# A decoder trunk's first norm: squares of a token-major copy on ScalarE in place of GpSimd's sums

## The chip, the cores and the metric

The kernel runs on one core of a Trainium2 chip. The metric is device time in microseconds (us): the median of three runs of the kernel before is 846.38 us (846.37 to 846.58). The engines are TensorE (PE, matmuls; PEld is its weight load), VectorE (DVE), ScalarE (ACT), GpSimd (POOL) and SyncE (SP), which issues most DMAs.

## The reference

One layer on x of 256 tokens by 2048 channels, all float32:

```
h = x * rsqrt(mean(x*x over channels) + 1e-6) * norm_w
proj = h @ w_in                     # 2048 x 14864: all inputs of three mixers, and gate logits
o_a, o_b, o_c = three token mixers of width 1024, each times silu of its own gate path
x = x + sum over n of sigmoid(gates[n]) * (o_n @ w_out[n])
out = rmsnorm(x, final_norm_w)
```

The change is in the first line: in how the mean of squares is made, and in how the scaled input gets to TensorE.

## The kernel before

**Numbers in two parts.** TensorE multiplies in float32r. So that float32 accuracy is kept, each operand is split: a high part (a cast to float32r) and a low part (the rest). A product takes three passes: high by high, high by low, low by high. For weights ScalarE casts (`whi<-raw`, L412) and VectorE subtracts (`wlo<-raw,whi`, L414), 1024 columns at a time; here such a half of a weight tile is called a step, h0, h1, h2 and so on. `split(h)` emits both, and once both halves of a tile are split the load of the tile three further on is issued on SP (`load`, L359): three buffers of 1 MB hold raw weights (`RB`), four hold split halves (`WB`), and `part(h)`, where TensorE takes step h, emits the split of step h + 3.

**The input.** `xT` is loaded channel-major into `xc_t`: 16 tiles of 128 channels by 256 tokens. `hT` holds x * norm_w in two parts, tile by tile; 1/rms is not in it, but is multiplied into results later (`rstd` along tokens in a row, `rtok` with tokens on partitions). `chunk(q)` makes four tiles of `hT`: ScalarE multiplies two of them and casts (ACTIVATE `hT<-xc_t,pr`), VectorE multiplies the other two into `boh`, ScalarE casts these, and VectorE makes the low parts: `low(k)` for the first two (SCALAR_TENSOR_TENSOR `hT<-xc_t,pr,hT`), one subtraction of 128x512 for the others (`hT<-boh,hT`). The first four tiles go by twos (`first_chunk`): a product and cast on ScalarE, and `low`, for each tile.

**The first block** (`chan_pair`) computes 512 columns of `w_in` (kind CC, inputs of the third mixer) in steps h0 to h7, eight of them, while the input still comes in; a step has 24 matmuls of 256 columns (L479). `squares(q)` is called in it for each quarter of the input: GpSimd squares four tiles and adds them up into `ssum`.

**The norm** (`norm_stream`): TensorE sums `ssum` over partitions, once with a matrix of ones (256 columns, the sum in all partitions) and twice into one column (tokens on partitions); ScalarE makes exp(-ln/2); VectorE refines it into `rstd`; GpSimd raises the column form to the power -1/2 (`rtok`).

**What sets the order.** Each engine executes its instructions in the order in which they were written. TensorE's blocks stand in a fixed order (`PLAN`); what is to be done between them (norm, mixers, emptying of accumulators) are generators, from which `Streams` takes pieces whenever a model of the engines' times (`Clock`, `Engine.cost`) says that a piece's inputs are there. So a change of one piece moves pieces behind it. A block's accumulators have two buffers (`pp`, `st.room()`): the third block needs those of the first, which `padded` empties, and that needs `rstd`. `branch_out(n)` holds the split outputs of a mixer (`boh`, `bol`), which the output projection of that mixer reads.

Of the kernel before, what the change touches and what calls it, by code (L numbers as in the profile page):

```python
# [281 lines left out]
def trunk(ctx, tc, xT, xtok, w, wdt, wax, prm, heads, cst, msk, fnw, out):  # L282
    nc = tc.nc
    PSUM = bass.MemoryType.PSUM
    consts = ctx.enter_context(tc.tile_pool(name="consts", bufs=1))
    big = ctx.enter_context(tc.tile_pool(name="big", bufs=1))
    wpool = ctx.enter_context(tc.tile_pool(name="wpool", bufs=WB))
    bop = ctx.enter_context(tc.tile_pool(name="bop", bufs=2))
# [24 lines left out]
    xc_t = big.tile([P, KD, S], F32, tag="x16", name="xc_t")  # L313
# [30 lines left out]
    def flag(name):  # L344
        flags[name] = max(ck.end, ck.after)
# [22 lines left out]
    x_there = []  # L368
# [29 lines left out]
    def split(h):  # L398
        if h >= 2 * NTILES or h in split_done:
            return  # L400
        split_done.add(h)
        raw = raws[h // 2]
        sl = slice((h % 2) * 1024, (h % 2) * 1024 + 1024)
        if h < LASTH:
            hi = wpool.tile([P, 1024], F32R, name="whi")
            lo = wpool.tile([P, 1024], F32R, name="wlo")
            ck.after = max(there[h], done.get(h - WB, 0.0))
        else:
            hi = fin["pool"].tile([P, 1024], F32R, name="whj", bufs=4)
            lo = fin["pool"].tile([P, 1024], F32R, name="wlj", bufs=4)  # L410
            ck.after = there[h]
        nc.scalar.copy(out=hi, in_=raw[:, sl])  # L412
        t = ck.run("act", 0.97)
        nc.vector.tensor_tensor(out=lo, in0=raw[:, sl], in1=hi.bitcast(F32), op=ALU.subtract)  # L414
        t = ck.run("dve", 1.15, t)
        parts[h] = (hi, lo, t)
        ck.after = ck.end = 0.0
        if h % 2:
            del raws[h // 2]
            load(h // 2 + RB, t)  # L420
            if h // 2 == 1:
# [17 lines left out]
    hT = big.tile([P, KD, 2, S], F32R, name="hT")  # L439
# [43 lines left out]
    def chan_pair():  # L483

        st.room()
        both = pp.tile([P, 2, 512], F32, name="ps")
        pss = [both[:, b].rearrange("p (c s) -> p c s", c=2) for b in range(2)]
        for u in (0, 1):
            first_split(u)
            first_chunk(u)  # L490
        split(1)
        chunk(1)
        for h in range(2, WB - 1):
            split(h)
        for q in range(4):
            for b in range(2):
                h = 2 * q + b
                if h in (5 - WB, 7 - WB):
                    chunk(2 + (h + WB - 5) // 2)
                hi, lo = part(h)  # L500
                if b == 0:
                    squares(q)
                ck.t["pe"] = max(ck.t["pe"], xs_at[q])
                first_quarter(pss[b], q, hi, lo, h)
        return pss
# [44 lines left out]

    rstd = consts.tile([P, 1, S], F32, name="rstd")
    rtok = consts.tile([P, 2, 2], F32, name="rtok")
    ssum = m1.tile([P, S], F32, tag="yg", name="ssum")
    rv = m1.tile([P, 2, S], F32, tag="br", name="rv")

    def chunk(q):

        x = xc_t[:, 4 * q:4 * q + 4]
        hi, lo = hT[:, 4 * q:4 * q + 4, 0], hT[:, 4 * q:4 * q + 4, 1]
        ck.after = x_there[q + 1]  # L560
        y = bop.tile([P, 2, S], F32, name="boh")
        for kk in range(2):
            act.activation(out=hi[:, kk], in_=x[:, kk], func=AF.Copy, scale=pc("norm_w", 4 * q + kk))
            dve.tensor_scalar(out=y[:, kk], in0=x[:, 2 + kk], scalar1=pc("norm_w", 4 * q + 2 + kk), scalar2=None, op0=ALU.mult)
        ck.after = ck.end
        act.copy(out=hi[:, 2:4], in_=y)
        for kk in range(2):
            low(4 * q + kk)
        ck.after = ck.end
        dve.tensor_tensor(out=lo[:, 2:4], in0=y, in1=hi[:, 2:4].bitcast(F32), op=ALU.subtract)  # L570
        xs_at[q] = ck.end
        ck.after = ck.end = 0.0

# [12 lines left out]
    def squares(q):
        x = xc_t[:, 4 * q:4 * q + 4]
        sq = bop.tile([P, 4, S], F32, name="bol")
        ck.after = x_there[q + 1]
        gpe.tensor_tensor(out=sq, in0=x, in1=x, op=ALU.mult)  # L590
        gpe.tensor_tensor(out=sq[:, 0:2], in0=sq[:, 0:2], in1=sq[:, 2:4], op=ALU.add)
        if q == 0:
            gpe.tensor_tensor(out=ssum, in0=sq[:, 0], in1=sq[:, 1], op=ALU.add)
        else:
            gpe.tensor_tensor(out=sq[:, 0], in0=sq[:, 0], in1=sq[:, 1], op=ALU.add)
            gpe.tensor_tensor(out=ssum, in0=ssum, in1=sq[:, 0], op=ALU.add)
        ck.after = ck.end = 0.0

    xs_at = {}

    def norm_stream():

        yield from st.get("pm", "p")
        ms = pm.tile([P, 512], F32, name="pmt")
        mm.matmul(ms[:, :S], lhsT=ones, rhs=ssum, start=True, stop=True)
        for j in range(2):
            mm.matmul(ms[:, S + j:S + j + 1], lhsT=ssum[:, j * P:(j + 1) * P], rhs=ones[:, 0:1], start=True, stop=True)
        yield "av"
        r0, v = rv[:, 0], rv[:, 1]
        act.activation(out=r0, in_=ms[:, :S], func=AF.Ln, scale=1.0 / D, bias=eps)  # L610
        act.activation(out=r0, in_=r0, func=AF.Exp, scale=-0.5)

        yield "v"
        dve.scalar_tensor_tensor(out=v, in0=ms[:, :S], scalar=D * EPS, in1=r0, op0=ALU.add, op1=ALU.mult)
        dve.tensor_scalar(out=rtok[:, 0], in0=ms[:, S:S + 2], scalar1=1.0 / D, scalar2=EPS, op0=ALU.mult, op1=ALU.add)
        st.put("pm")
        dve.scalar_tensor_tensor(out=v, in0=v, scalar=-0.5 / D, in1=r0, op0=ALU.mult, op1=ALU.mult)
        dve.scalar_tensor_tensor(out=rstd[:, 0], in0=v, scalar=1.5, in1=r0, op0=ALU.add, op1=ALU.mult)
        flag("rstd")
        half = m1.tile([P, 2], F32, name="half")  # L620
        gp.memset(half, -0.5)
        gp.tensor_tensor(out=rtok[:, 0], in0=rtok[:, 0], in1=half, op=ALU.pow)
        gp.tensor_scalar(out=rtok[:, 1], in0=rtok[:, 0], scalar1=0.5, scalar2=None, op0=ALU.mult)
        flag("rtok")


    rcoef = consts.tile([P, 8], F32, name="rcoef")
# [828 lines left out]
```

## Time and profile before

| | |
|---|---|
| median of 3 runs | 846.38 us |
| profiled execution | 848.2 us, of which its span (first to last instruction) 846.4 us |
| mean granted clock of TensorE | 0.994 |
| TensorE busy | 827.4 us, 98% of the span, 4953 matmuls |
| VectorE, ScalarE, GpSimd busy | 637.3, 475.2, 35.9 us |
| DMA | 159.08 MB, mean 188 GB/s |

Times in rows are from the span's start. A row of the timeline may merge equal instructions that follow each other (xN); its square bracket is the idle time before it and what ended it. Matmuls overlap, so their pace is read from starts. [...] The last 14.3 us of the span are the end of the final norm and the output's DMAs.

### The profile page before, as it was taken

How to read it: one execution, taken by the hardware profiler on the slowest of the kernel's cores; microseconds unless marked ns; L12 is line 12 of the kernel's file. 1: busy time of each engine (PE TensorE's matmuls, PEld its weight loads, DVE VectorE, ACT ScalarE, POOL GpSimd, SP SyncE). 2: the span in 40 equal slices, each digit the busy share in tenths (PEclk: the TensorE clock that was granted, in tenths of full speed). 3: DMA queues.
4: the chain of work that ended last, by engine and by line, in shares of the span. 5: the costliest groups of instructions: out<-in, count | busy, mean ns of one | idle time of the engine just before them, and what ended most of it. 6: DMA issues, size and time to landing. Idle time of an engine off the chain costs nothing.

```text
span 846.4 us, 12476 instructions
## 1 busy us (share of the span) xinstructions
PE 827.4 (98%) x4953; PEld 702.1 (83%) x4953; DVE 637.3 (75%) x961; ACT 475.2 (56%) x647; POOL 35.9 (4%) x58
## 2 busy tenths in 40 slices
PE   6899999999999999999999999999999999999995
PEld 6888888878888888888888888888888888888885
DVE  7978888787879768668668778778878877566463
ACT  4466455645564755746656556746656665544443
POOL 6301000000000000000100000000000000000000
PEclk9999999999999999999999999999999999999998
DMA  8537564754545545554554445545544554655532
GB/s 302 197 127 256 173 218 150 310 181 168 199 168 194 203 185 195 199 198 150 204 196 180 171 150 202 196 151 199 180 169 155 194 198 151 248 192 179 195 131 100
DMA packets 24618, 159.08 MB, mean 188 GB/s; under 512 B 2816, under 2 KB 3360, under 8 KB 6768
## 3 DMA queue, kind: packets, MB, share of 16 engines
q1 hardware_dynamic: 23072, 151.53, 50.1%
q0 software_dynamic: 1344, 6.67, 2.3%
q8 instruction: 39, 0.64, 0.3%
q10 hardware_dynamic: 144, 0.09, 0.1%
q14 instruction: 19, 0.16, 0.1%
HBM read 156.16 MB, written 2.11 MB: 187 GB/s over the span
## 4 chain that ended last, share of the span: by engine, by line
PE 95%; DVE 2%; issue 1%; DMA 1%; ACT 0%; POOL 0%; POOLq 0%; SPq 0%; DVEq 0%; ACTq 0%
PE ps L466 25%; PE ps L519 17%; PE ps L521 17%; PE ps L520 17%; PE ps L467 12%; PE pmt L158 3%; PE ps L479 2%; DVE wlo L414 1%; PE pmt L946 1%; DVE boh L158 1%; DVE hT L158 1%; DMA xc_t<-xT 1%; PE pmt L748 0%; PE ps L539 0%; PE ps L537 0%
## 5 line engine op out<-in xcount | busy, mean ns | idle before, releaser
L414 DVE TENSOR_TENSOR wlo<-raw,whi 128x1024 fp32r<-128x1024 f32 x275 | 337.1, 1231 | 163.6 <-ACT whi L412 162.9
L412 ACT CAST whi<-raw 128x1024 fp32r<-128x1024 f32 x275 | 288.3, 1051 | 298.0 <-PE ps L521 146.3
L466 PE MATMUL ps<-hT,whi 128*128 128x512 f32 x896 | 318.2, 399 | 0.0
L467 PE MATMUL ps<-hT,wlo 128*128 128x256 f32 x896 | 251.1, 280 | 0.0
L466 PEld LDWEIGHTS ps<-hT,whi 128*128 128x128 f32 x896 | 168.3, 188 | 41.6 <-issue 1.0
L519 PE MATMUL ps<-whi,hT 128*128 128x512 f32 x448 | 175.2, 391 | 0.0
L520 PE MATMUL ps<-wlo,hT 128*128 128x512 f32 x448 | 174.5, 389 | 0.0
L521 PE MATMUL ps<-whi,hT 128*128 128x512 f32 x448 | 174.4, 389 | 0.0
L467 PEld LDWEIGHTS ps<-hT,wlo 128*128 128x128 f32 x896 | 169.1, 189 | 0.5
L521 PEld LDWEIGHTS ps<-whi,hT 128*128 128x128 f32 x448 | 84.1, 188 | 17.8
L519 PEld LDWEIGHTS ps<-whi,hT 128*128 128x128 f32 x448 | 84.1, 188 | 17.4 <-issue 0.3
L520 PEld LDWEIGHTS ps<-wlo,hT 128*128 128x128 f32 x448 | 84.1, 188 | 16.6
L519 PE MATMUL ps<-whi,boh 128*128 128x512 f32 x176 | 69.8, 397 | 0.0
L521 PE MATMUL ps<-whi,bol 128*128 128x512 f32 x176 | 68.7, 390 | 0.0
L520 PE MATMUL ps<-wlo,boh 128*128 128x512 f32 x176 | 68.5, 389 | 0.0
L521 PEld LDWEIGHTS ps<-whi,bol 128*128 128x128 f32 x176 | 33.0, 188 | 7.1
L519 PEld LDWEIGHTS ps<-whi,boh 128*128 128x128 f32 x176 | 33.0, 188 | 6.7
L520 PEld LDWEIGHTS ps<-wlo,boh 128*128 128x128 f32 x176 | 33.1, 188 | 6.5
L131 ACT ACT_TABLE_LOAD x26 | 33.4, 1283 | 1.6 <-PEq L1449 1.2
L479 PE MATMUL ps<-hT,whi 128*128 128x256 f32 x128 | 20.1, 309 | 8.3 <-ACT whi L412 4.9
L479 PEld LDWEIGHTS ps<-hT,whi 128*128 128x128 f32 x128 | 18.1, 212 | 9.9 <-ACT whi L412 5.3
L158 ACT ACTIVATE gt<-ps,rtok 128x512 f32<-128x512 f32 x24 | 15.6, 684 | 7.0 <-PE ps L521 6.9
(250 smaller groups left out, 687.2 us busy)
## 6 DMA issues: line engine op xcount, KB each, us to landing
raw<-w SPq DMA_DIRECT2D x137, 1024.0 KB, 4.8
raw<-w SPq DMA_DIRECT2D x5, 512.0 KB, 8.9
brd<-sums POOLq DMA_DIRECT2D x4, 512.0 KB, 6.7
xacc<-xtok POOLq DMA_DIRECT2D x1, 2048.0 KB, 12.6
out_dram<-xacc SPq DMA_DIRECT2D x7, 256.0 KB, 2.4
xc_t<-xT SPq DMA_DIRECT2D x3, 512.0 KB, 9.8
wx<-wax POOLq DMA_DIRECT2D x4, 256.0 KB, 3.4
fw<-fnw POOLq DMA_DIRECT2D x1, 1024.0 KB, 5.3
```

Of the source, the lines that this page charges most:

```text
L131: self.eng.preload_act_table_set(self.set)
L158: return f(*a, **k)
L412: nc.scalar.copy(out=hi, in_=raw[:, sl])
L414: nc.vector.tensor_tensor(out=lo, in0=raw[:, sl], in1=hi.bitcast(F32), op=ALU.subtract)
L466: pe.matmul(ps[:, ct], lhsT=hi[:, c0:c0 + 128], rhs=flat(hT[:, k]), start=k == 0, stop=False)
L467: pe.matmul(ps[:, ct, S:], lhsT=lo[:, c0:c0 + 128], rhs=hT[:, k, 0], start=False, stop=k == KD - 1)
L479: pe.matmul(ps[:, ct], lhsT=(hi, lo)[i][:, c0:c0 + 128], rhs=hT[:, q * 4 + kk, j], start=q == 0 and n == 0, stop=q == 3 and n == last)
L519: pe.matmul(pss[j], lhsT=hi_ap(k, j), rhs=hi[:, sl], start=k == 0, stop=False)
L520: pe.matmul(pss[j], lhsT=hi_ap(k, j), rhs=lo[:, sl], start=False, stop=False)
L521: pe.matmul(pss[j], lhsT=lo_ap(k, j), rhs=hi[:, sl], start=False, stop=k == nk - 1)
L946: pe.matmul(o, lhsT=wp[:, a, ct, g], rhs=xp[:, b, ct], start=u == 0, stop=u == 2)
```

## The change

A copy of x with tokens on partitions (`xsq`, two tiles of 128x2048, 1 MB each) is loaded on SP, behind the fifth weight tile and three small constants, into buffers that the branch outputs use later (`bol`). In `norm_stream` ScalarE squares each and sums along its channels, VectorE adds epsilon, GpSimd makes the power -1/2 and half of it (`rtok`), VectorE multiplies the identity by each column (`dg`), and one matmul of ones by `dg` puts 1/rms of all tokens into all partitions; VectorE copies it to `rstd`. `squares`, `ssum`, the ln and exp and the refinement are gone. In `chunk` every tile now is one ScalarE product with cast and one VectorE `low`.

```diff
@@ split(), behind the load of the fifth weight tile
                 nc.sync.dma_start(out=cs[:, :EARLY], in_=cst[:, :EARLY])
                 nc.sync.dma_start(out=hp, in_=heads)
                 nc.sync.dma_start(out=wd, in_=wdt)
+                for j in range(2):
+                    nc.sync.dma_start(out=xsq[j], in_=xtok[:, j])
+                    dma[0] += 2.9
@@ chan_pair()
                 hi, lo = part(h)
-                if b == 0:
-                    squares(q)
                 ck.t["pe"] = max(ck.t["pe"], xs_at[q])
@@
-    ssum = m1.tile([P, S], F32, tag="yg", name="ssum")
-    rv = m1.tile([P, 2, S], F32, tag="br", name="rv")
+    xsq = [bop.tile([P, D], F32, tag="bol", name="xsq") for _ in range(2)]
@@ chunk(q)
-        y = bop.tile([P, 2, S], F32, name="boh")
-        for kk in range(2):
-            act.activation(out=hi[:, kk], in_=x[:, kk], func=AF.Copy, scale=pc("norm_w", 4 * q + kk))
-            dve.tensor_scalar(out=y[:, kk], in0=x[:, 2 + kk], scalar1=pc("norm_w", 4 * q + 2 + kk), scalar2=None, op0=ALU.mult)
-        ck.after = ck.end
-        act.copy(out=hi[:, 2:4], in_=y)
-        for kk in range(2):
-            low(4 * q + kk)
-        ck.after = ck.end
-        dve.tensor_tensor(out=lo[:, 2:4], in0=y, in1=hi[:, 2:4].bitcast(F32), op=ALU.subtract)
+        for k in range(4 * q, 4 * q + 4):
+            act.activation(out=hT[:, k, 0], in_=xc_t[:, k], func=AF.Copy, scale=pc("norm_w", k))
+        for k in range(4 * q, 4 * q + 4):
+            low(k)
@@ norm_stream()
...
+        yield "a"
+        ss = consts.tile([P, 2], F32, name="ss")
+        for j in range(2):
+            act.activation(out=xsq[j], in_=xsq[j], func=AF.Square, accum_out=ss[:, j:j + 1])
+        yield "v"
+        dve.tensor_scalar(out=rtok[:, 0], in0=ss, scalar1=1.0 / D, scalar2=EPS, op0=ALU.mult, op1=ALU.add)
+        half = m1.tile([P, 2], F32, name="half")
+        gp.memset(half, -0.5)
+        gpe.tensor_tensor(out=rtok[:, 0], in0=rtok[:, 0], in1=half, op=ALU.pow)
+        gpe.tensor_scalar(out=rtok[:, 1], in0=rtok[:, 0], scalar1=0.5, scalar2=None, op0=ALU.mult)
+        flag("rtok")
+        yield "v"
+        dg = m1.tile([P, 2, P], F32, tag="br", name="dg")
+        for j in range(2):
+            dve.tensor_scalar(out=dg[:, j], in0=ident, scalar1=rtok[:, 0, j:j + 1], scalar2=None, op0=ALU.mult)
+        yield from st.get("pm", "p")
+        ms = pm.tile([P, 512], F32, name="pmt")
+        mm.matmul(ms[:, :S], lhsT=ones, rhs=flat(dg), start=True, stop=True)
+        yield "v"
+        dve.tensor_copy(out=rstd[:, 0], in_=ms[:, :S])
+        st.put("pm")
+        flag("rstd")
@@ where the streams start
-            st.add(norm_stream(), ck.t["pool"])
+            st.add(norm_stream(), dma[0])
```

How the instructions stand now. First VectorE in the first block, before (`wlo` are remainders of weight steps, `boh` its products, `hT` low parts):

```order
L414 TENSOR_TENSOR wlo<-raw,whi 128x1024
L158 TENSOR_SCALAR boh<-xc_t,pr 128x256 x2
L158 SCALAR_TENSOR_TENSOR hT<-xc_t,pr,hT 128x256 x2
L158 TENSOR_TENSOR hT<-boh,hT 128x2x256
L414 TENSOR_TENSOR wlo<-raw,whi 128x1024 x2
```

and the same place now, from the remainder of h1 on:

```order
L414 TENSOR_TENSOR wlo<-raw,whi 128x1024
L158 SCALAR_TENSOR_TENSOR hT<-xc_t,pr,hT 128x256 x4
L414 TENSOR_TENSOR wlo<-raw,whi 128x1024 x2
L158 SCALAR_TENSOR_TENSOR hT<-xc_t,pr,hT 128x256 x4
L414 TENSOR_TENSOR wlo<-raw,whi 128x1024 x2
```

The two products and the difference of each chunk are gone, and four low parts stand in one row. Second, TensorE behind the first block, before (L479 are the block's last passes, L519 to L521 the triples of the next block):

```order
L479 MATMUL ps<-hT,wlo 128x256 x8
L519 MATMUL ps<-whi,hT 128x512
L520 MATMUL ps<-wlo,hT 128x512
L521 MATMUL ps<-whi,hT 128x512
L158 MATMUL pmt<-ssum,ones 128x256
L158 MATMUL pmt<-ones,ssum 128x1 x2
L519 MATMUL ps<-whi,hT 128x512
```

and where the norm's one matmul stands now, in the same block (its lines are L520 to L522 now):

```order
L521 MATMUL ps<-wlo,hT 128x512
L522 MATMUL ps<-whi,hT 128x512
L158 MATMUL pmt<-dg,ones 128x256
L520 MATMUL ps<-whi,hT 128x512
L521 MATMUL ps<-wlo,hT 128x512
```

The norm's matmul moved from behind the first triple to behind the twenty-sixth, and the two of one column are gone. Third, VectorE where the third mixer's output is finished, before (`csq` are its sums of squares, `rv` and `crs` its 1/rms, `yg` the output, `bol` its low part, which the output projection reads):

```order
L158 TENSOR_TENSOR csq<-csq 128x256
L414 TENSOR_TENSOR wlo<-raw,whi 128x1024
L158 TENSOR_TENSOR cpad<-cpad,ps 128x2x256
L158 TENSOR_TENSOR cpad<-cpad,rstd 128x2x256
L414 TENSOR_TENSOR wlo<-raw,whi 128x1024
L158 SCALAR_TENSOR_TENSOR rv<-pmt,crs 128x256
L158 SCALAR_TENSOR_TENSOR rv<-rv,crs 128x256
L158 SCALAR_TENSOR_TENSOR crs<-rv,crs 128x256
L158 SCALAR_TENSOR_TENSOR yg<-yg,snwh,crs 128x256 x4
L414 TENSOR_TENSOR wlo<-raw,whi 128x1024 x2
L158 TENSOR_TENSOR bol<-yg,boh 128x1024
```

and now:

```order
L158 TENSOR_TENSOR csq<-csq 128x256
L414 TENSOR_TENSOR wlo<-raw,whi 128x1024 x2
L158 SCALAR_TENSOR_TENSOR rv<-pmt,crs 128x256
L158 SCALAR_TENSOR_TENSOR rv<-rv,crs 128x256
L158 SCALAR_TENSOR_TENSOR crs<-rv,crs 128x256
L158 SCALAR_TENSOR_TENSOR yg<-yg,snwh,crs 128x256 x4
L414 TENSOR_TENSOR wlo<-raw,whi 128x1024 x2
L158 TENSOR_TENSOR bol<-yg,boh 128x1024
```

This output is now written behind the remainder of step h73, where before it was h66; its first use, at step h72, has not moved in TensorE's order. The emptying of another block (`cpad`) no longer stands in between.

## Rows read from the trace of the kernel before

**Rows 1.** Stretches: start:end, length, busy us per engine (instructions), PEclk, DMA share, GB/s

```profile
6.15:42.64 36.49, 28.13 (x192) 26.55 (x193) 34.17 (x30) 16.49 (x24) 21.61 (x16) 0.95 0.69 260
42.64:832.10 789.46, 789.46 (x4699) 666.19 (x4698) 595.35 (x908) 451.90 (x611) 12.29 (x34) 1.00 0.52 185
20.00:25.00 5.00, 2.88 (x22) 2.52 (x21) 5.00 (x4) 0.00 (x0) 4.84 (x4) 1.00 0.02 7
30.00:35.00 5.00, 5.00 (x32) 5.00 (x31) 4.76 (x9) 3.13 (x6) 0.00 (x0) 0.66 0.28 83
```

**Rows 2.** Timeline of TensorE, 0 to 45: start, length, instructions, idle before

```profile
6.15 2.08 PE L479 MATMUL ps<-hT,whi 128*128 128x256 f32 x8 [0.91 <-ACT hT L158]
...
8.88 1.05 PE L479 MATMUL ps<-hT,whi 128*128 128x256 f32 x4
10.88 0.50 PE L479 MATMUL ps<-hT,whi 128*128 128x256 f32 x2 [0.95 <-DVE hT L158]
...
12.57 2.07 PE L479 MATMUL ps<-hT,whi 128*128 128x256 f32 x16
...
29.55 2.60 PE L479 MATMUL ps<-hT,whi 128*128 128x256 f32 x16 [2.43 <-ACT whi L412]
...
36.88 2.08 PE L479 MATMUL ps<-hT,whi 128*128 128x256 f32 x16
...
43.77 0.50 PE L158 MATMUL pmt<-ones,ssum 128*128 128x1 f32 x4
```

**Rows 3.** Groups on VectorE, 7 to 29.4: busy us, mean ns, idle before

```profile
L158 DVE SCALAR_TENSOR_TENSOR hT<-xc_t,pr,hT 128x256 fp32r<-128x256 f32 x7 | 7.8, 1142 | 0.0
L414 DVE TENSOR_TENSOR wlo<-raw,whi 128x1024 fp32r<-128x1024 f32 x3 | 6.3, 2137 | 0.0
...
L435 DVE TENSOR_TENSOR wlo<-raw,whi 128x512 fp32r<-128x512 f32 x1 | 2.4, 2384 | 0.0
```

**Rows 4.** The same view of VectorE, 30.2 to 44.2

```profile
L414 DVE TENSOR_TENSOR wlo<-raw,whi 128x1024 fp32r<-128x1024 f32 x8 | 9.4, 1219 | 2.6 <-ACT whi L412 2.6
L158 DVE TENSOR_TENSOR hT<-boh,hT 128x512 fp32r<-128x512 f32 x2 | 1.4, 679 | 0.0
L158 DVE SCALAR_TENSOR_TENSOR hT<-xc_t,pr,hT 128x256 fp32r<-128x256 f32 x2 | 0.9, 472 | 0.0
```

**Rows 5.** Timeline of ScalarE, first block

```profile
9.47 1.04 ACT L412 CAST whi<-raw 128x1024 fp32r<-128x1024 f32 x1 [1.66 <-DMA raw<-w]
11.18 0.91 ACT L158 ACTIVATE hT<-xc_t,pr 128x256 fp32r<-128x256 f32 x2 [0.67 <-DMA xc_t<-xT]
...
33.65 3.89 ACT L412 CAST whi<-raw 128x1024 fp32r<-128x1024 f32 x4
```

**Rows 6.** Timeline of SP's queue, first block

```profile
7.05 0.47 SPq L375 DMA_DIRECT2D xc_t<-xT  x1
14.57 10.42 SPq L359 DMA_DIRECT2D raw<-w  x2
```

**Rows 7.** DMA issues of 7.05 and 14.57: KB, us to landing

```profile
xc_t<-xT SPq DMA_DIRECT2D x1, 512.0 KB, 11.7
...
raw<-w SPq DMA_DIRECT2D x1, 1024.0 KB, 6.7
```

**Rows 8.** Timeline of TensorE around 206 and 239

```profile
206.06 0.60 PE L158 MATMUL pmt<-csq,ones 128*128 128x256 f32 x2
...
238.76 0.39 PE L519 MATMUL ps<-whi,boh 128*128 128x512 f32 x1
...
239.44 0.39 PE L519 MATMUL ps<-whi,boh 128*128 128x512 f32 x1
```

**Rows 9.** Timeline of ScalarE around 202

```profile
202.20 1.06 ACT L158 ACTIVATE csq<-yg 128x1024 f32<-128x1024 f32 x1
```

**Rows 10.** Timeline of GpSimd around 46

```profile
45.97 0.81 POOL L622 TENSOR_TENSOR rtok<-rtok,half 128x2 f32<-128x2 f32 x1 [16.52 <-DVE rtok L158]
```

**Rows 11.** Timeline of VectorE around 215

```profile
215.20 1.22 DVE L158 TENSOR_TENSOR bol<-yg,boh 128x1024 fp32r<-128x1024 f32 x1
```

More of the change, by code (lines that the diff above doesn't have):

```diff
@@ L552, in trunk @@
     rtok = consts.tile([P, 2, 2], F32, name="rtok")
-    ssum = m1.tile([P, S], F32, tag="yg", name="ssum")
-    rv = m1.tile([P, 2, S], F32, tag="br", name="rv")
+    xsq = [bop.tile([P, D], F32, tag="bol", name="xsq") for _ in range(2)]
     def chunk(q):
-        x = xc_t[:, 4 * q:4 * q + 4]
-        hi, lo = hT[:, 4 * q:4 * q + 4, 0], hT[:, 4 * q:4 * q + 4, 1]
         ck.after = x_there[q + 1]
-        y = bop.tile([P, 2, S], F32, name="boh")
-        for kk in range(2):
-            act.activation(out=hi[:, kk], in_=x[:, kk], func=AF.Copy, scale=pc("norm_w", 4 * q + kk))
-            dve.tensor_scalar(out=y[:, kk], in0=x[:, 2 + kk], scalar1=pc("norm_w", 4 * q + 2 + kk), scalar2=None, op0=ALU.mult)
-        ck.after = ck.end
-        act.copy(out=hi[:, 2:4], in_=y)
-        for kk in range(2):
-            low(4 * q + kk)
-        ck.after = ck.end
-        dve.tensor_tensor(out=lo[:, 2:4], in0=y, in1=hi[:, 2:4].bitcast(F32), op=ALU.subtract)
+        for k in range(4 * q, 4 * q + 4):
+            act.activation(out=hT[:, k, 0], in_=xc_t[:, k], func=AF.Copy, scale=pc("norm_w", k))
+        for k in range(4 * q, 4 * q + 4):
+            low(k)
         xs_at[q] = ck.end
@@ L584, in first_chunk @@
         ck.after = ck.end = 0.0
[L586 to L597, printed above, removed]
@@ L603, in norm_stream @@
+        gpe.tensor_scalar(out=rtok[:, 1], in0=rtok[:, 0], scalar1=0.5, scalar2=None, op0=ALU.mult)
[4 more added lines that the diff above has]
+            dve.tensor_scalar(out=dg[:, j], in0=ident, scalar1=rtok[:, 0, j:j + 1], scalar2=None, op0=ALU.mult)
         yield from st.get("pm", "p")
         ms = pm.tile([P, 512], F32, name="pmt")
-        mm.matmul(ms[:, :S], lhsT=ones, rhs=ssum, start=True, stop=True)
@@ L606, in norm_stream @@
[L606 to L611, printed above, removed]
+        mm.matmul(ms[:, :S], lhsT=ones, rhs=flat(dg), start=True, stop=True)
         yield "v"
-        dve.scalar_tensor_tensor(out=v, in0=ms[:, :S], scalar=D * EPS, in1=r0, op0=ALU.add, op1=ALU.mult)
@@ L615, in norm_stream @@
-        dve.tensor_scalar(out=rtok[:, 0], in0=ms[:, S:S + 2], scalar1=1.0 / D, scalar2=EPS, op0=ALU.mult, op1=ALU.add)
+        dve.tensor_copy(out=rstd[:, 0], in_=ms[:, :S])
         st.put("pm")
-        dve.scalar_tensor_tensor(out=v, in0=v, scalar=-0.5 / D, in1=r0, op0=ALU.mult, op1=ALU.mult)
-        dve.scalar_tensor_tensor(out=rstd[:, 0], in0=v, scalar=1.5, in1=r0, op0=ALU.add, op1=ALU.mult)
         flag("rstd")
-        half = m1.tile([P, 2], F32, name="half")
-        gp.memset(half, -0.5)
@@ L622, in norm_stream @@
-        gp.tensor_tensor(out=rtok[:, 0], in0=rtok[:, 0], in1=half, op=ALU.pow)
-        gp.tensor_scalar(out=rtok[:, 1], in0=rtok[:, 0], scalar1=0.5, scalar2=None, op0=ALU.mult)
-        flag("rtok")
     rcoef = consts.tile([P, 8], F32, name="rcoef")
```

## The prediction

> **What bounds the kernel now.** I read the stretches first: what TensorE does in each part of the span. From 42.64 to 832.10 us it is busy for 789.46 of 789.46 us [rows 1]: behind the first block nothing ever holds it, so work taken from another engine there is worth nothing. The ends are the 14.3 us behind 832.10, where the last rows leave, and the start, 0 to 42.64 us. The first block runs from 6.15 to 42.64, 36.49 us, with TensorE busy for 28.13 of it. Next comes the timeline of TensorE [rows 2]. The block is eight steps, h0 to h7, of 24 passes over 1024 weight columns; undisturbed a step takes (42.64 - 36.88) / 2 = 2.88 us, so eight need 23.0 us, and 13.5 us are lost. [...]
>
> Then who is late: VectorE. Between 7 and 29.4 us its remainder of 128x1024 takes 2137 ns and its low half of 128x256 1142 ns [rows 3]; between 30.2 and 44.2 the same forms take 1219 and 472 [rows 4]. What ends at 29.4 is GpSimd's sum of squares: GpSimd is busy for 4.84 of the 5 us from 20 to 25 [rows 1]. It isn't the transfers: in the same 5 us their share is 0.02, and VectorE is as slow. Everything else is behind VectorE: the chunk's cast on ScalarE waits for its products, and the next weight tile's load for its remainders.
>
> **The change part by part.**
>
> GpSimd's sixteen operations go, and VectorE gets its own pace back. Of each later chunk (4 tiles) VectorE does four low halves, about 4 x 0.45 us, in place of two products, two low halves and one 128x512 difference; ScalarE does four products in place of two products and a cast. The product no longer goes from VectorE to ScalarE and back. I lay the start out again by row durations.
>
> Landings don't move. ScalarE's waits for h1's weights and for tiles 4 to 7 ended just before 9.47 and 11.18 [rows 5]; the last start piece was issued at 7.05 and took 11.7 us, 18.75 [rows 6, 7]. Six pieces of 512 KB lie between, 1.27 us each: weights of h2 12.4, h3 13.7, tiles 8 to 11 15.0, h4 16.2, h5 17.5, tiles 12 to 15 18.8. The fourth weight tile, issued at 14.57, landed 6.7 us later, 21.3 [rows 6, 7]; it was in line behind these, so an earlier issue doesn't bring it.
>
> ScalarE, with 0.455 us a product and 0.97 a cast [rows 5]: h1 9.47 to 10.5, four products 11.2 to 13.0, casts of h2 and h3 to 14.0 and 15.0, products to 16.85, h4 17.85, h5 18.8, products to 20.7, h6 (landed 21.3) 22.3, h7 23.3. VectorE at its own pace [rows 4]: from 7.03 on the second half of h0's remainder (0.68 in place of 2.38 [rows 3, 4]) and the low halves of tiles 2 and 3, ready at 8.6; h1's remainder 11.75, tiles 4 to 7 13.45, h2 15.25, h3 16.45, tiles 8 to 11 18.1, h4 19.3, h5 20.5, tiles 12 to 15 22.2, h6 23.6, h7 24.8.
>
> TensorE: up to 8.88 as before. Then twelve passes of h0; between 9.9 and 12.57 the passes got twice as fast, and as it is at least as busy up to there I keep the middle, 11: ten passes at 0.215 and two at 0.12, h0 ends at 11.3 (before, 12.57). h1 to 14.2. h2 asks for its cast at 14.2, there since 14.0, and for its remainder at 16.1 (15.25); h3 at 17.05, h4 19.9, h5 22.8, h6 25.7, h7 28.6 find theirs. The block ends at 11.3 + 7 x 2.88 = 31.45 in place of 42.64: 11.2 us less, with the half-clock stretch of 30 to 35 inside that, as no gap is left to bring it. The tightest place is h2, 0.2 us, and it also caps the gain: had the clock risen at 9.9, TensorE would wait there for ScalarE, whose two added products (0.9 us) stand ahead of that cast. So this is worth 11.0 to 11.4.
>
> The norm's matmuls: before, one of 256 columns and two of one column; now the one of 256 alone. The single-column ones took four passes in 0.50 us [rows 2], on a TensorE that is the bound: 0.4 us less; between 0.2 and 0.5.
>
> Two loads of 1 MB (the token-major copy) enter SP's queue behind the constants and ahead of the sixth weight tile, and every later load. That tile's first use is the third step behind the block, at 31.45 + 2 x 2.72 = 36.9 (a triple of 512 columns takes 239.44 - 238.76 = 0.68 us, four to a step [rows 8]). The fifth tile is now issued when h3's remainder is done, 16.45, and not near 25 [rows 6], so the stream doesn't stop: at 2.5 us a MB 23.8 for the fifth, 25.1 with the constants, 30.1 with the two copies, 32.6 the sixth; cast and remainder (1.05 + 1.22) make 34.9. Spare 2.0: cost 0. The other bound is the mean of the whole block, 260 GB/s [rows 1], 4.0 us a MB: sixth tile at 39.5, its remainder at 41.8, 4.9 us of waiting. That mean holds the five empty us from 20 to 25; the pace of the full queue is nearer, so 0 it is. [...]
>
> The two squares of 2048 elements are put behind h13's cast on ScalarE, near 38 us. One of 1024 takes 1.06 us [rows 9], so 2.0 each, to 42. Queued behind them is h14's cast, needed with its remainder by 31.45 + 6 x 2.72 = 47.8 and ready at 44.3: hidden. If it weren't, the whole 4 us would show.
>
> 1/rms now comes late. VectorE scales, GpSimd's power takes 0.81 us [rows 10], VectorE makes the diagonal behind h15's remainder, 46.4. The matmul stands 26 triples behind the block in TensorE's order, at 49.1: spare 2.7. The copy and the two products that empty the block's accumulators end near 52; the block that takes them over starts 32 triples and the time-step matmuls later, past 53.2: spare over 1 us. Cost 0, at most 2.
>
> So the mixers' work starts some 15 us later against TensorE. What is late next: the third branch's output. Before, its sum of squares reached TensorE at 206.06, the last half was written at 216.4, and first used at 238.76 [rows 8, 11]: 22 us spare. Now TensorE's order has 17 triples, 11.6 us, between that matmul and the first use, and the chain took 10.4: 1.2 us spare. Cost 0 to 2; I take 0, as VectorE has less in between (no input of the next block).
>
> Sum: 6.15 + 25.3 + (789.46 - 0.4) + 14.3 = 834.8 us of span. Against the profiled execution (848.2, of which the span is 846.4) that is 836.6; against the median of 846.38, 11.6 less, **834.8 us**.
>
> **Rivals.**
>
> *Only half is won (20%).* The start finds another holder: ScalarE now carries all products and stands 0.2 us ahead at h2, the copies share the transfers, and one gap near 2 us would bring a half-clock stretch back (the one seen cost 0.34 of 5 us, 1.7). With 1 to 3 us of gaps and that, the gain is 7 to 9: 837.4 to 839.4. For: ScalarE's small spare. Against: every later step has 2 us or more.
>
> *The third branch or 1/rms holds TensorE once (10%).* The start gains as forecast, and 1 to 3 us go back where the spares are 1 us: 835.8 to 837.8. Against: 790 us without one wait in the old order.
>
> *VectorE stays slow (3%)*, its pace having been the transfers' doing: about 846. Against: 20 to 25 us.
>
> *Slower: the clock doesn't rise (3%).* [...]
>
> **How the numbers follow.** The forecast has 64%, its own range 834.2 to 836. Below, h2's cap and the 0.5 us of the small matmuls leave nothing under about 834.2; I go to 833.6 for what the row durations leave open. Above, the first two rivals and the dear bound of the copies (834.8 + 4.9) reach up to 839.5 before 2 in 10 are out. Within 0.2% (1.7 us, what a measurement of this kernel can tell) lies the slow VectorE: 3%; slower is the clock, 3%; faster 94%.
>
> **What would show it.** Right: GpSimd idle from 1 to 40 us; VectorE's 128x1024 near 1.22 us from the start; TensorE without a gap over 0.3 us from 6.15 on, the block's end at 31 to 32; no half clock behind 12; the sixth tile landed by 33; the norm's matmul unwaited near 49; the first use of the third branch unwaited. Wrong: a wait of TensorE on ScalarE at h2 to h5, on a weight load at the third step behind the block, or behind 200 us; VectorE stretched without GpSimd; a later block end at the same gaps, which would be the clock.

## The result, and the profile after

The changed kernel takes **836.09 us** (median of 4 runs, 835.72 to 836.33), against 846.38 before: 10.3 us less, a ratio of 0.9877 (95% interval 0.9866 to 0.9889). The forecast was 834.8, its range 833.6 to 839.5; its own narrower range ended at 836, 0.1 below the median. The profiled execution took 836.15 us (forecast for that one: 836.6), its span 834.4 (834.8).

The stretches, with the columns of [rows 1] (PEclk is the clock that TensorE was granted, as a share of full speed): the first block, the rest up to the last matmuls, and three stretches that answer to those of before.

```profile
5.76:30.82 25.06, 25.06 (x192) 24.82 (x193) 17.72 (x27) 15.86 (x25) 0.00 (x0) 1.00 1.01 401
30.82:819.80 788.98, 788.98 (x4696) 666.11 (x4695) 595.68 (x909) 456.00 (x614) 13.17 (x34) 1.00 0.53 187
...
6.15:42.64 36.49, 36.49 (x245) 34.20 (x244) 22.94 (x36) 25.34 (x39) 0.00 (x0) 1.00 0.94 369
20.00:25.00 5.00, 5.00 (x44) 5.00 (x43) 3.60 (x6) 3.22 (x5) 0.00 (x0) 1.00 1.02 411
30.00:35.00 5.00, 5.00 (x28) 4.28 (x27) 1.22 (x2) 2.26 (x4) 0.00 (x0) 1.00 1.01 416
```

The block takes 25.06 us instead of 36.49 and TensorE is busy for all of it. Behind it nothing waits, as before. From 20 to 25 GpSimd, busy for 4.84 us before, does nothing, VectorE has time left over, and the transfers, which stood still there [rows 1], run at 411 GB/s. The clock is full from 30 to 35.

The groups of VectorE from 7 to 29.4 us, for [rows 3]:

```profile
L414 DVE TENSOR_TENSOR wlo<-raw,whi 128x1024 fp32r<-128x1024 f32 x9 | 10.7, 1222 | 3.9 <-ACT whi L412 3.9
L158 DVE SCALAR_TENSOR_TENSOR hT<-xc_t,pr,hT 128x256 fp32r<-128x256 f32 x14 | 5.9, 480 | 0.0
L438 DVE TENSOR_TENSOR wlo<-raw,whi 128x512 fp32r<-128x512 f32 x1 | 0.7, 691 | 0.0
```

The forms that took 2137, 1142 and 2384 ns take 1222, 480 and 691, the pace that [rows 4] showed without GpSimd's sums; and it is VectorE now that waits for ScalarE (3.9 us).

TensorE's timeline, for [rows 2] and [rows 8]: steps h1 and h2, the end of the block, the norm's matmul, the first use of the third branch's low part.

```profile
5.76 2.07 PE L482 MATMUL ps<-hT,whi 128*128 128x256 f32 x8 [0.53 <-ACT hT L158]
...
10.43 2.17 PE L482 MATMUL ps<-hT,whi 128*128 128x256 f32 x16
...
13.45 2.17 PE L482 MATMUL ps<-hT,whi 128*128 128x256 f32 x16
...
30.82 0.40 PE L520 MATMUL ps<-whi,hT 128*128 128x512 f32 x1
...
48.54 0.59 PE L158 MATMUL pmt<-dg,ones 128*128 128x256 f32 x2
...
225.80 0.39 PE L522 MATMUL ps<-whi,bol 128*128 128x512 f32 x1
```

Only the first row has a bracket, 0.53 us ahead of the block. Of the 13.5 us that the old block lost, 25.06 - 23.04 = 2.0 are left: passes at the start that take almost twice as long (eight in 2.07 us at 5.76, but sixteen in 2.17 at 10.43; before, the four that start at 8.02 take 0.215 us each up to 8.88). That this is a lower clock was my reading, in the prediction too, and isn't shown: the granted clock reads 1.00 from 1 to 12 us before and after, and 1.00 up to 12 us in e8 as well, where the first eight take 1.43 us.

ScalarE's timeline, for [rows 5] and [rows 9]: the casts of h2 and h3, of the sixth weight tile (h10, h11), the two squares, and h14's cast.

```profile
12.37 2.02 ACT L412 CAST whi<-raw 128x1024 fp32r<-128x1024 f32 x2
...
32.70 2.01 ACT L412 CAST whi<-raw 128x1024 fp32r<-128x1024 f32 x2 [6.78 <-DMA raw<-w]
...
37.61 1.92 ACT L158 ACTIVATE xsq<-xsq 128x2048 f32<-128x2048 f32 x1
...
39.51 1.90 ACT L158 ACTIVATE xsq<-xsq 128x2048 f32<-128x2048 f32 x1
...
41.51 1.98 ACT L412 CAST whi<-raw 128x1024 fp32r<-128x1024 f32 x2
```

VectorE's timeline, for [rows 11]: h10's and h11's remainders, the diagonal, the third branch's low part.

```profile
33.78 2.36 DVE L414 TENSOR_TENSOR wlo<-raw,whi 128x1024 fp32r<-128x1024 f32 x2 [6.42 <-ACT whi L412]
...
45.64 0.48 DVE L158 TENSOR_SCALAR dg<-cs,rtok 128x128 f32<-128x128 f32 x2
...
222.34 1.22 DVE L158 TENSOR_TENSOR bol<-yg,boh 128x1024 fp32r<-128x1024 f32 x1
```

### The profile page after: what moved, and what is told of

The parts are those of the page before. It is cut to its first block, busy times and chain, and to the rows that moved or that the text cites. A ratio compares the mean times of both kernels' runs of the same rounds, so it can differ in the third digit from the quotient of the medians.

```text
span 834.4 us, 12450 instructions
## 1 busy us (share of the span) xinstructions
PE 823.8 (99%) x4949; PEld 700.2 (84%) x4949; DVE 621.1 (74%) x958; ACT 478.6 (57%) x652; POOL 15.2 (2%) x43
## 4 chain that ended last, share of the span: by engine, by line
PE 98%; issue 1%; DMA 0%; DVE 0%; ACT 0%; POOL 0%; POOLq 0%; SPq 0%; DVEq 0%; ACTq 0%
PE ps L469 25%; PE ps L520 17%; PE ps L522 17%; PE ps L521 17%; PE ps L470 13%; PE pmt L158 3%; PE ps L482 3%; PE pmt L926 1%; DMA xc_t<-xT 0%; PE pmt L728 0%; PE ps L540 0%; PE ps L538 0%; PE ps L539 0%; DVE xacc L158 0%; PE pmt L1153 0%
## 5 line engine op out<-in xcount | busy, mean ns | idle before, releaser
L469 PEld LDWEIGHTS ps<-hT,whi 128*128 128x128 f32 x896 | 168.2, 188 | 41.2 <-issue 1.0
L520 PE MATMUL ps<-whi,hT 128*128 128x512 f32 x448 | 175.3, 391 | 0.0
L521 PE MATMUL ps<-wlo,hT 128*128 128x512 f32 x448 | 174.5, 389 | 0.0
L522 PE MATMUL ps<-whi,hT 128*128 128x512 f32 x448 | 174.4, 389 | 0.0
L522 PEld LDWEIGHTS ps<-whi,hT 128*128 128x128 f32 x448 | 84.1, 188 | 17.7
L520 PEld LDWEIGHTS ps<-whi,hT 128*128 128x128 f32 x448 | 84.1, 188 | 17.6 <-issue 0.3
L521 PEld LDWEIGHTS ps<-wlo,hT 128*128 128x128 f32 x448 | 84.1, 188 | 16.7
L520 PE MATMUL ps<-whi,boh 128*128 128x512 f32 x176 | 69.8, 397 | 0.0
L522 PE MATMUL ps<-whi,bol 128*128 128x512 f32 x176 | 68.7, 390 | 0.0
L521 PE MATMUL ps<-wlo,boh 128*128 128x512 f32 x176 | 68.5, 389 | 0.0
L522 PEld LDWEIGHTS ps<-whi,bol 128*128 128x128 f32 x176 | 33.0, 188 | 7.1
L520 PEld LDWEIGHTS ps<-whi,boh 128*128 128x128 f32 x176 | 33.0, 188 | 6.6
L521 PEld LDWEIGHTS ps<-wlo,boh 128*128 128x128 f32 x176 | 33.1, 188 | 6.4
L482 PE MATMUL ps<-hT,whi 128*128 128x256 f32 x128 | 18.4, 298 | 0.5 <-ACT hT L158 0.5
L158 DVE SCALAR_TENSOR_TENSOR gt<-gt,ps 128x512 f32<-128x512 f32 (+1 forms) x25 | 16.5, 659 | 3.0 <-PE ps L540 2.4
```

The costliest lines, as they stand in the source:

```text
L158: return f(*a, **k)
L469: pe.matmul(ps[:, ct], lhsT=hi[:, c0:c0 + 128], rhs=flat(hT[:, k]), start=k == 0, stop=False)
L482: pe.matmul(ps[:, ct], lhsT=(hi, lo)[i][:, c0:c0 + 128], rhs=hT[:, q * 4 + kk, j], start=q == 0 and n == 0, stop=q == 3 and n == last)
L520: pe.matmul(pss[j], lhsT=hi_ap(k, j), rhs=hi[:, sl], start=k == 0, stop=False)
L521: pe.matmul(pss[j], lhsT=hi_ap(k, j), rhs=lo[:, sl], start=False, stop=False)
L522: pe.matmul(pss[j], lhsT=lo_ap(k, j), rhs=hi[:, sl], start=False, stop=k == nk - 1)
```

## The experiments

**Theory A**: the gain is the sums' going. GpSimd's operations, which read SBUF, stretch VectorE's operations, VectorE is late for TensorE, and TensorE's waits are the 10 us; the new chunk and the new norm's own work count for little. **Rivals**: the new chunk (two products and a difference less on VectorE) carries a good part; or GpSimd's being busy matters, whatever it does; or it is the sums' work, wherever it stands.

### Which part carries the gain

*e1, the new chunk alone.* The kernel before with this edit; sums and old norm stay:

```diff
@@ chunk(q)
-        y = bop.tile([P, 2, S], F32, name="boh")
...
-        dve.tensor_tensor(out=lo[:, 2:4], in0=y, in1=hi[:, 2:4].bitcast(F32), op=ALU.subtract)
+        for k in range(4 * q, 4 * q + 4):
+            act.activation(out=hT[:, k, 0], in_=xc_t[:, k], func=AF.Copy, scale=pc("norm_w", k))
+        for k in range(4 * q, 4 * q + 4):
+            low(k)
```

> The new chunk alone: one ScalarE product and one VectorE low half for each tile; GpSimd's sums and the old norm stay. Theory A (GpSimd's sums, which read SBUF, stretch VectorE): VectorE's 128x1024 remainder still takes about 2 us until GpSimd ends near 28, the first block ends at 37 to 41, time 840 to 845. Theory B (the gain comes from the chunk's own work and from the product no longer going from VectorE to ScalarE and back): the block ends near 32, time 836 to 838.

Measured: 845.1 us, just above A's 840 to 845; ratio 0.9987 (0.9978 to 0.9996), against 846.4. VectorE from 7 to 29.4, and two of TensorE's waits:

```profile
L158 DVE SCALAR_TENSOR_TENSOR hT<-xc_t,pr,hT 128x256 fp32r<-128x256 f32 x11 | 13.4, 1270 | 0.0
L414 DVE TENSOR_TENSOR wlo<-raw,whi 128x1024 fp32r<-128x1024 f32 x4 | 8.6, 2176 | 0.0
```

```profile
20.20 0.50 PE L479 MATMUL ps<-hT,whi 128*128 128x256 f32 x2 [1.53 <-DVE hT L158]
22.41 2.08 PE L479 MATMUL ps<-hT,wlo 128*128 128x256 f32 x8 [1.71 <-DVE wlo L414]
```

VectorE is as slow as before, and TensorE still waits for it. What the smaller chunk saves is 1.3 us.

*e2 and e12, the new norm alone.* The changed kernel with the old chunk (the diff above, reversed), run twice, the second time beside e11, the changed kernel again on the same chip:

> The new norm alone: the token-major copy, the squares on ScalarE, no sums on GpSimd; the chunk is the old one. Theory A: VectorE's 128x1024 takes 1.22 us from the start, the first block ends at 31 to 33, time 836 to 838. Theory B: the waits between VectorE's products and ScalarE's casts stay, the block ends at 37 or later, time 842 to 846.

> The changed norm with the old chunk again, on the same chip as the changed kernel. If the chunk's part is worth anything once the sums are gone, it is above the changed kernel by the two waits seen in its first look, 0.3 us or more: 836.4 to 836.8. If it is worth nothing: equal within 0.2 us.

> The changed kernel, unchanged, on the same chip as the next one: 836.1, 835.8 to 836.4.

Measured: e2 836.38 us (ratio 0.9881, 0.9864 to 0.9897); e12 836.02 (835.76 to 836.33) and e11 836.33 (836.17 to 836.38), on one chip. The second pair puts the norm alone level with the changed kernel: 0.3 us on the other side, just outside the 0.2 expected for no difference, and too little to tell apart here. With the sums gone the chunk's edit is worth nothing. Its 1.3 us in e1 and its nothing here don't add up to a share of its own: it saves VectorE time, and that seems to count only while VectorE is late.

### What about the sums costs the time

*e3, the sums back, unread.* The changed kernel with the 15 GpSimd operations of the sums before, in the same place:

```diff
@@ chan_pair()
+                if b == 0:
+                    squares(q)
@@ ahead of norm_stream()
+    ssum = m1.tile([P, S], F32, tag="yg", name="ssum")
+
+    def squares(q):
+        x = xc_t[:, 4 * q:4 * q + 4]
+        sq = bop.tile([P, 4, S], F32, name="boh")
+        gp.tensor_tensor(out=sq, in0=x, in1=x, op=ALU.mult)
+        gp.tensor_tensor(out=sq[:, 0:2], in0=sq[:, 0:2], in1=sq[:, 2:4], op=ALU.add)
...
```

> The changed kernel with GpSimd's sixteen sum operations put back, their result read by nobody. Theory A: VectorE is stretched again (128x1024 at about 2 us, 128x256 low half over 1 us) and the time goes back to 840 to 845. Theory B: GpSimd's work is off the path, 836 to 837.

Measured: 844.5 us, ratio 0.998 (0.9971 to 0.9989). VectorE from 7 to 29.4, the largest of GpSimd's operations, and the stretch 12 to 18:

```profile
L158 DVE SCALAR_TENSOR_TENSOR hT<-xc_t,pr,hT 128x256 fp32r<-128x256 f32 x10 | 13.0, 1350 | 0.0
L414 DVE TENSOR_TENSOR wlo<-raw,whi 128x1024 fp32r<-128x1024 f32 x4 | 8.6, 2176 | 0.0
L438 DVE TENSOR_TENSOR wlo<-raw,whi 128x512 fp32r<-128x512 f32 x1 | 2.4, 2392 | 0.0
```

```profile
L585 POOL TENSOR_TENSOR boh<-xc_t 128x1024 f32<-128x1024 f32 x4 | 8.1, 2028 | 6.0 <-DMA xc_t<-xT 6.0
```

```profile
12.00:18.00 6.00, 6.00 (x39) 6.00 (x39) 6.00 (x5) 5.78 (x9) 5.76 (x5) 0.72 1.03 421
```

Work whose result nobody reads gives 8.4 of the 10.3 us back, and every duration of [rows 3] with it, at a transfer share of 1.03: VectorE was slow without transfers in [rows 1] (20 to 25) and is slow here with them, so they aren't the cause. (The other 1.9 us are near the chunk's 1.3 of e1 and the 0.5 of the norm's small matmuls.) Not all of it is waiting, as theory A had it. The first block runs from 6.13 to 40.30 here, 34.17 us; TensorE is idle for 5.3 of them, and the granted clock is 0.72 from 12 to 18, 0.81 from 20 to 25 and 0.85 from 25 to 30, which costs 0.28 x 6 + 0.19 x 5 + 0.15 x 5 = 3.4 us more.

*e4, GpSimd as busy, but writing only.* In place of `squares`, twenty memsets of 128x1024:

```diff
+        for n in range(5):
+            gp.memset(sq, float(n))
```

> The changed kernel with twenty GpSimd memsets of 128x1024 in the first block, their result read by nobody: GpSimd is busy for about 20 us and reads nothing. Theory A, with the reading as its cause: VectorE keeps 1.22 us for 128x1024, time 836 to 837. Rival W (any GpSimd instruction holds VectorE): VectorE stretched as with the sums, 840 to 845.

Measured: 835.89 us, ratio 0.9875 (0.986 to 0.989). VectorE from 7 to 29.4, and GpSimd's timeline:

```profile
L414 DVE TENSOR_TENSOR wlo<-raw,whi 128x1024 fp32r<-128x1024 f32 x9 | 10.7, 1223 | 5.2 <-ACT whi L412 5.2
L158 DVE SCALAR_TENSOR_TENSOR hT<-xc_t,pr,hT 128x256 fp32r<-128x256 f32 x14 | 5.9, 482 | 0.1
```

```profile
0.91 19.82 POOL L583 MEMSET boh<- 128x1024 f32 x20
```

GpSimd is busy up to 20.7 us and VectorE keeps its pace. So it isn't the engine's being busy. The same VectorE form takes 2176 ns beside the sums, which read (e3), and 1223 beside the memsets, which only write.

*e8 and e13, one input in place of two.* The memset of e4 becomes a product of `x` with a number (128x1024, one SBUF input), twenty of them in e8 and eight in e13 (`range(2)`):

```diff
+        for n in range(5):
+            gp.tensor_scalar(out=sq, in0=x, scalar1=float(n), scalar2=None, op0=ALU.mult)
```

> The changed kernel with twenty more GpSimd operations in the first block, each a product of a 128x1024 piece of the input with a number, result unread: one input from SBUF in place of the two that the old sums had. Theory A (whatever GpSimd reads from SBUF stretches VectorE): VectorE's 128x1024 remainder well above 1.22 us in the first block, the block ends several us later, 840 to 845. Rival B (only operations of GpSimd with two SBUF inputs do it): 1.22 us, 835.5 to 836.6.

> The same one-input products as e8, but eight in place of twenty: at 3.26 us each they end near 33, so GpSimd is busy for the whole first block and free again ten us before its power is wanted at 44. If e8's 27 us were the wait for that power and nothing else (Rival B): the changed kernel's time, 835.7 to 836.6, block end at 31.2. If one-input reads cost VectorE's pace too: above 838.

Measured: e8 863.0 us, 1.0193 (1.0178 to 1.0208), a miss for both; e13 835.84, 0.9875 (0.9858 to 0.9891). In e8 the first block ends at 31.22, and nearly all of the loss is one wait, 24.86 of 26.5 us of span; TensorE's timeline, and GpSimd's:

```profile
31.22 0.40 PE L522 MATMUL ps<-whi,hT 128*128 128x512 f32 x1
...
73.94 1.22 PE L158 MATMUL pmt<-dg,ones 128*128 128x256 f32 x2 [24.86 <-DVE dg L158]
```

```profile
7.22 65.11 POOL L584 TENSOR_SCALAR boh<-xc_t 128x1024 f32<-128x1024 f32 x20 [6.24 <-DMA xc_t<-xT]
...
72.56 0.72 POOL L158 TENSOR_TENSOR rtok<-rtok,half 128x2 f32<-128x2 f32 x1
```

At 65.11 / 20 = 3.26 us each (I had thought of the 2 us that the two-input form takes) they stood ahead of the power in GpSimd's queue, and so ahead of 1/rms: an error of the experiment, not a cost of reading. e13 keeps the queue short. VectorE from 7 to 29.4, and GpSimd:

```profile
L414 DVE TENSOR_TENSOR wlo<-raw,whi 128x1024 fp32r<-128x1024 f32 x9 | 11.3, 1302 | 1.2 <-ACT whi L412 1.2
L158 DVE SCALAR_TENSOR_TENSOR hT<-xc_t,pr,hT 128x256 fp32r<-128x256 f32 x14 | 9.0, 696 | 0.0
```

```profile
7.06 30.64 POOL L584 TENSOR_SCALAR boh<-xc_t 128x1024 f32<-128x1024 f32 x8 [6.09 <-DMA xc_t<-xT]
```

GpSimd reads SBUF during the whole block; VectorE's low half goes from 480 to 696 ns, its remainder from 1222 to 1302, and the time is that of the changed kernel: VectorE's spare holds the stretch, and TensorE is idle for 0.89 us in all from 6 to 30. (It was expected that a stretch of VectorE would show as 838 or more.) So the cost goes by degrees: a remainder takes 1222 ns with GpSimd silent, 1302 beside these products, 2176 beside the sums (e3). What is not told apart: whether the sums do more because they have two inputs, or because they read faster (1024 elements from each input in 2.03 us, against 3.8 us here).

*e10, the same sums, later.* The kernel before with the new chunk; ScalarE releases the sums behind h10's cast, when the first block is done:

```diff
@@ chan_pair()
-                if b == 0:
-                    squares(q)
...
+        for q in range(4):
+            squares(q)
@@ squares(q)
-        ck.after = x_there[q + 1]
+        ck.after = max(x_there[q + 1], ck.t["pe"])
+        if q == 0:
+            act.copy(out=sq[:, 0, 0:1], in_=ones[:, 0:1])
```

> The kernel before, with the changed chunk, and its sums kept but held until the first block is done: the same GpSimd work and the same old norm, in a stretch where VectorE has spare time. Theory A (the sums cost only through VectorE's pace in the first block): the block ends near 31 to 32, VectorE's 128x1024 remainder is stretched to 2 us or more behind it, and what is left is a wait of TensorE for 1/rms, which now comes late: 837 to 842. Rival B (the sums cost the same wherever they stand, or the gain came from something else than their place): 845 or more.

Measured: 846.69 us, ratio 1.0001 (0.9992 to 1.0011): no gain. A's number is missed and B's, 845 or more, is met; the rows tell by what. TensorE's timeline, and the stretch 56 to 66:

```profile
31.20 0.40 PE L519 MATMUL ps<-whi,hT 128*128 128x512 f32 x1
...
56.23 1.22 PE L158 MATMUL pmt<-ssum,ones 128*128 128x256 f32 x2 [3.76 <-POOL half L615]
...
61.89 0.80 PE L466 MATMUL ps<-hT,whi 128*128 128x512 f32 x1 [2.30 <-ACT vt L158]
```

```profile
56.00:66.00 10.00, 7.46 (x22) 5.89 (x23) 6.75 (x15) 3.10 (x5) 1.39 (x7) 0.50 0.26 97
```

The block ends at 31.20, as A said, with GpSimd silent up to 29.1. But the sums now end at 56.2, 27 us later than before, 1/rms with them, and TensorE waits 3.76 and 2.30 us; and from 56 to 66 its clock is at half, so that 7.46 us of work cost 3.7 more than at full. 6.1 + 3.7 is nearly all that had been won. I had priced the wait and not the clock behind it. So it isn't that the sums cost the same wherever they stand, though the times are alike. Moving the sums isn't enough: the new route to 1/rms is what lets them go.

### The prices of what was added

*e6, two copies more.* Two further loads of the token-major copy, ahead of the sixth weight tile:

```diff
+                for j in (0, 1):
+                    nc.sync.dma_start(out=spare[j], in_=xtok[:, j])
...
```

> The changed kernel with two more loads of 1 MB (the copy a second time, read by nobody) ahead of the sixth weight tile. If the spare of the sixth tile is what the landings say (32.6, with cast and remainder 34.9, first use at 36.3), 5 us more make 39.9 and TensorE waits about 3.6 us at the third step behind the block: 839 to 840. If loads are hidden by far more than that: 836 to 837.

Measured: 841.64 us, ratio 0.9944 (0.993 to 0.9957), some 2 us more than expected. TensorE's waits, and the stretch behind them:

```profile
38.65 0.50 PE L522 MATMUL ps<-whi,hT 128*128 128x512 f32 x1 [2.02 <-ACT whi L412]
...
39.91 0.50 PE L523 MATMUL ps<-wlo,hT 128*128 128x512 f32 x1 [0.76 <-DVE wlo L414]
```

```profile
41.00:44.50 3.50, 3.50 (x10) 2.71 (x9) 2.80 (x7) 3.50 (x5) 0.00 (x0) 0.51 0.74 248
```

5 us more of transfers bring 2.8 us of waiting at the step named in the prediction, so the spare there is about 2; and 3.5 us at a clock of 0.51 behind it cost 1.7. Together they are 4.5 of the 4.8 us by which this execution's span (839.2) is the longer one.

*e7, two squares more* on ScalarE, in `norm_stream`:

```diff
...
+        for j in range(2):
+            nc.scalar.activation(out=spare[j], in_=xsq[j], func=AF.Square, accum_out=ss2[:, j:j + 1])
```

> The changed kernel with two more squares of 128x2048 on ScalarE ahead of the norm's own, read by nobody: 3.8 us more on ScalarE near 38 us. By the spares of the changed kernel's trace (h14's remainder ready at 43.8, used at 47.1; the norm's matmul ready near 46.1, run at 48.5) TensorE waits 1 to 2.5 us once: 837 to 839. If ScalarE's work there is hidden altogether: 836 to 836.5.

Measured: 838.11 us, ratio 0.9901 (0.9887 to 0.9914), as expected. TensorE's timeline, behind the first block:

```profile
47.88 0.50 PE L521 MATMUL ps<-wlo,hT 128*128 128x512 f32 x1 [0.18 <-DVE wlo L414]
...
50.19 0.70 PE L158 MATMUL pmt<-dg,ones 128*128 128x256 f32 x2 [0.87 <-DVE dg L158]
```

3.8 us more on ScalarE bring 1.05 us of waits, at h14 and at the norm's matmul: the first pair is hidden, with under 3 us to spare. (This span, 836.4, is 2.0 us the longer. Of these 1.65 stand at the norm's matmul, 50.19 against 48.54: the block's end is 0.14 later, and the two waits, with the passes beside them, make most of the rest. The last 0.35 come behind it, and what makes them isn't shown.)

*e5, the kernel before, unchanged*, profiled again for the half-clock stretch in [rows 1]:

> The kernel before, unchanged, for its spread: its profiled execution took 848.2 us, its median is 846.38, and the changed kernel's are 836.15 and 836.09. Theory A2: the profiled execution lost 1.7 us to a half-clock stretch (granted 0.66 in 30 to 35 us) that most executions don't have, so executions at 846.4 have a mean granted clock of 0.996 or more, against 0.994. Rival: the profile itself costs some 1.8 us in the kernel before, and the clock is 0.994 in all.

Measured: 846.13 us (11 runs, 845.97 to 846.54), ratio 0.9997. This time the profiled execution took 846.33, its span 844.6. Its stretch 30 to 35, and the end of its first block:

```profile
30.00:35.00 5.00, 4.47 (x35) 4.26 (x36) 4.75 (x9) 2.08 (x3) 0.00 (x0) 1.00 0.28 79
```

```profile
40.98 0.40 PE L519 MATMUL ps<-whi,hT 128*128 128x512 f32 x1
```

The clock is full, and the block ends 1.66 us earlier than in the execution that the prediction was read from (42.64), with as much waiting in it (8.9 us up to there against 9.3). A2's own sign failed all the same: of the 11 executions only two had a mean granted clock of 0.996 or more, and three, at 845.98 to 846.54 us, had 0.992, less than the 0.994 of the one at 848.2. (That mean takes in the end behind the last matmul, where the clock is at 0.50 too: 840 to 846.4, before.) The rival failed as well: this profiled execution took no 1.8 us more than the others. Where the 1.66 lie is seen in TensorE's timeline of e5, h4 and h6:

```profile
28.24 1.70 PE L479 MATMUL ps<-hT,whi 128*128 128x256 f32 x12 [1.82 <-ACT whi L412]
...
35.22 2.08 PE L479 MATMUL ps<-hT,whi 128*128 128x256 f32 x16
```

h4 begins 1.31 us earlier than at 29.55 [rows 2], ahead of the half-clock stretch. From there to h6 it takes 6.98 us, against 7.33 with the stretch: only 0.35 us less, since at full clock TensorE waits for VectorE in h4 (0.20 and 0.39 us).

## Why the prediction was right, and where it was off

- **What bounds the kernel**: right. The gain lies in the first block, 36.49 us to 25.06; of the rest, 789.46 became 788.98.
- **VectorE gets its pace back**: right, and the cause is shown: e3 brings the stretch back with the sums alone, e4 doesn't.
- **The block's end**: 31.45 forecast, 30.82 measured. 0.39 of the difference is the start (5.76, not 6.15), the rest the block's length, 25.3 against 25.06. What sets the moment at which the passes get faster is shown by no run (11 was an estimate): h0 ended at 10.43 where 11.3 was forecast, in e4 the first eight were fast already. The cap was where it was put: h2's cast, 1.01 us behind 12.37, is ready as TensorE begins h2 at 13.45. In e4, e7 and e10 the early passes were faster (the first eight in 1.43 us, not 2.07), and TensorE waited 0.3 to 0.7 us for that cast, as the prediction said. What it didn't see is that h1's cast caps the start too: 1.18 us of waiting in e4, and in e8 0.39 there and none at h2. TensorE's timeline of e4, first pass, h1 and h2:

```profile
5.75 1.43 PE L482 MATMUL ps<-hT,whi 128*128 128x256 f32 x8 [0.51 <-ACT hT L158]
...
10.33 2.17 PE L482 MATMUL ps<-hT,whi 128*128 128x256 f32 x16 [1.18 <-ACT whi L412]
...
13.79 2.18 PE L482 MATMUL ps<-hT,whi 128*128 128x256 f32 x16 [0.32 <-ACT whi L412]
```

- **Small matmuls**: 0.4 forecast, 0.48 measured for the whole rest (789.46 - 788.98).
- **Copies at 0**: right. The sixth tile was there by 32.70, where its cast starts (32.6 forecast); its first remainder ended near 35.0 (34.9), and the step's first use came at 36.3 (36.9): 1.3 spare, not 2.0, as the block ended earlier. Priced by e6 it is near 2. Transfers ran at 411 and 416 GB/s (20 to 25, 30 to 35).
- **Squares at 0, 1/rms late but in time**: right. Squares from 37.61 (38 forecast), diagonal ready at 46.1 (46.4), matmul at 48.54 (49.1): 2.4 spare against 2.7, and e7 finds it.
- **Third branch at 0**: right. Its low part is written by 223.6 and first used at 225.80, 2.2 spare where 1.2 was forecast.
- **The mis-sized term** is the last step, "against the median of 846.38, 11.6 less". The 11.6 were worked out in an execution of 848.2 us, 1.8 above the median, and taken from the median. e5 is an execution at the median: its block ends at 40.98, not 42.64, and 844.6 - 834.4 = 10.2 us of span, the 10.3 of the medians. The prediction names the half-clock stretch that the long execution held ("with the half-clock stretch of 30 to 35 inside that") and prices it at 1.7. e5 shows it worth 0.35 beside the waits that take its place; the other 1.31 of the 1.66 lie ahead of it, in a start that differs from execution to execution. The profiled execution's own time, 836.6, was forecast to 0.5 us.
- **One reading** was wrong, without weight in the sum. The sums are fifteen operations; the sixteenth that [rows 1] counts is a memset of `half`.
- **Rivals**: "only half is won" wanted a gap near 2 us at the start; there was none (the profile after has no wait in the block, e11 an idle TensorE for 1.2 us in all from 6 to 12). e6 and e10 show what it feared: TensorE waits (2.02 us, 3.76 us), and a stretch at a granted clock of 0.51 and 0.50 follows. That the slow pace of the start lasts through the block ("the clock doesn't rise") is shown by no run: after, sixteen passes take 2.17 us at 10.43.

The chunk's edit, which took most working in the layout of ScalarE and VectorE, turned out to be worth nothing measurable beside the norm's (e2, e12). No run was below the changed kernel by a measurable amount.

## What to carry to other kernels

Before an engine's durations are used as prices, compare the same form in two stretches of the trace: here VectorE's remainder took 2137 ns up to the end of GpSimd's sums and 1219 behind them, and the going of the sums was worth 8.4 of the 10.3 us (e3), where the work taken from VectorE itself was worth nothing measurable (e12). A gain that is read from one profiled execution is set against that execution; where it stands above the median, look for what only it holds before the difference is carried over. Work that is moved off the start must be followed to its next reader: the same sums, moved behind the first block, left the time at 846.69 us (e10), through a later 1/rms and the half clock behind that wait.

## What the runs showed of the hardware

- GpSimd's product of 128x1024 with a number took 3.80 us in e13, from 7 to 38 us, with VectorE busy for 21.4 of the 24 us from 6 to 30, and 2.8 for the last nine of the twenty in e8 ((63.6 - 38.6) / 9), with VectorE idle from 48 to 66; its two-input product of the same size took 2.03 beside a busy VectorE (e3): the form with less to read is the slower one, and the stretch goes both ways.
- VectorE's product of one tile with a number from a column (`boh<-xc_t,pr`, in the kernel before) is stretched most of all by the sums, 1418 ns against 340, though it reads one tile and not two. The windows are those of [rows 3] and [rows 4]:

```profile
L158 DVE TENSOR_SCALAR boh<-xc_t,pr 128x256 f32<-128x256 f32 x4 | 5.5, 1418 | 0.0
...
L158 DVE TENSOR_SCALAR boh<-xc_t,pr 128x256 f32<-128x256 f32 x2 | 0.6, 340 | 0.0
```

- The clock's fall is not settled by the waits alone: two executions of the kernel before, with 9.3 and 8.9 us of waits in the start (the longest 2.48 and 2.65), had 3.4 us at half clock behind them (0.51 from 31 to 34.4) and none (1.00 throughout). In the first, the clock stayed full behind the wait of 2.48 us (1.00 from 18.29 to 24) and fell behind that of 2.43. What decides it stays open.
